# Linear attention in a fused decoder trunk: one of four projection blocks as a plain product, weight sums formed by accumulating loads, no weight split on GpSimd, gate activations issued later

## The chip, the cores and the metric

The kernel runs on one core of a Trainium2 chip. The metric is the time of one execution on the device in microseconds (us). A core has five engines with a queue each, which are named here as the profile names them: PE (matrix products; PEld are its weight loads), DVE (vector engine), ACT (scalar engine), POOL (GpSimd) and SP, which only issues transfers. POOL and ACT issue transfers too, and a transfer that adds to what lies at its destination is issued by POOL here. Each engine works its queue in order; an instruction that waits for a semaphore holds up all that stands behind it on its engine.

## The reference

Two layers on a sequence of 512 tokens, model width 1024, float32: latent attention and an MLP, then gated linear attention and an MLP, and a last norm. The change concerns the linear attention alone:

```python
def gla_mixer(xn, w_in, w_gk_up, b_gk, g_norm, w_o):
    h = xn @ w_in                       # w_in: 1024 x 3088
    q = h[..., :512]; k = h[..., 512:1024]          # 4 heads of 128
    v = h[..., 1024:2048]; g = h[..., 2048:3072]    # 4 heads of 256
    gk = log_sigmoid(h[..., 3072:] @ w_gk_up + b_gk) / 16
    ...                                 # chunks of 64, decays exp(cumsum(gk))
    o = rms_norm(o, g_norm)
    o = o * silu(g)
    return o.reshape(B, S, 1024) @ w_o
```

`...` stands for the recurrence over chunks: products of queries with the state, of queries with keys under the decay, and the new state.

## The kernel before, in words

Every matrix operand in float32 is cut into a high and a low part, and a product is three PE passes (high·high, high·low, low·high). The cut of a weight piece of 128x1024 is two instructions: ACT copies the high part (tile `wh`, line L124), and the difference (tile `wl`, L127) is a subtraction with two inputs from on-chip memory, on DVE or, where `lo_eng=POOL` is given, on POOL. `piece` (L164) does both.

The linear attention (`gla`, from L1243) computes the columns of q, k, v and g from the normed input X. The columns of v and g come in four blocks of 512 columns: v for heads 0 and 1 (called "v"), g for heads 0 and 1 ("g"), then "V" and "G" for heads 2 and 3. Before, each block is done by `b_type` with seven quadrant products in place of eight (Strassen's scheme in Winograd's form): the input and the weight are halved in both directions, sums of input quadrants (T1 to T4) are formed once by `quadrants` (L1257), and sums of weight quadrants for each block. A quadrant product (`product`, L1307) is 24 matmuls of 256 columns, all at L1314. The weight quadrants lie in four rooms of 128x1024: a11, s1, a12 and s3. Two of the four weight sums are formed while loading: SP loads one quadrant (L1303) and POOL then loads another on top of it (L1305). The other two are formed on DVE: a11 becomes s1 + a11 (L1344), a12 becomes a11 + a12 (L1355). Of the seven cuts of a block, four have their subtraction on DVE and three on POOL (`cut_in(a12, POOL)`, `cut_in(s3, POOL)`, `cut_in(a22, POOL)`). `copied` (L1317) and `added` (L1322) put the partial results together in the order that the scheme needs.

`v_done` (L1481, L1482) scales v by the row norms and cuts it; `g_done` (L1390) collects g in tiles and then, right at the end of the block, runs the eight gate activations (Silu, L1395) on ACT at high priority. They need another function table than the rest, so a table load stands ahead of them and one behind.

Two lists of work are woven into each other by hand (`proj` and `heads`, driven by the loop at the end of `gla`): `proj` yields units of main work (a product counts 0.7, a q or k column piece 2), and for every unit the loop takes 1.27 steps of `heads`. A step is a stage of the decay products of two heads (`levels`: on DVE the products L1542, L1574, L1575 and the masked copies L1559, L1561, L1584; on PE L1549 and L1599), or of `states`, `own_tiles`, `past` and `gated`, which form the outputs. For heads 0 and 1 the levels fall into "v" and "g", and states and outputs into the q and k pieces of the other two heads; for heads 2 and 3 the levels fall into "V" and "G", and the rest behind them. Then comes the output projection (`out_start`, `out_proj`), whose first three tiles need all heads.

The order on each engine is settled when the program is built; the PE order, above all, is fixed, so PE waits at a product whose operand is late even if a later one could run.

Of the kernel before, what the change touches and what calls it, by code (L numbers as in the profile page):

```python
# [18 lines left out]
P = 128  # L19
D = 1024  # L20
# [30 lines left out]
def trunk_kernel(ctx: ExitStack, tc: tile.TileContext, t_in: dict, out: bass.AP):  # L51
# [112 lines left out]
    def piece(raw, a, n, order=lambda i: i, at=(W_AT, W_AT), lo_eng=DVE):  # L164
        hi = room_for("wh", a, n, at[0])
        lo = room_for("wl", a, n, at[1])
        split(raw, hi, lo, lo_eng=lo_eng, order=order)
        return hi, lo
# [1074 lines left out]
    def gla(layer, nrm, vtag, ytag):  # L1243
# [13 lines left out]
        def quadrants():  # L1257
# [6 lines left out]
            sums = [[f(slot(vtag)) for _ in range(2)] for _ in range(4)]  # L1264
            t1, t2, t3, t4 = ([two[k // 2][:, k % 2 * TH : (k % 2 + 1) * TH] for k in lead] for two in sums)
            for k in lead:
                g1, g2 = (gcol(nrm.g, nrm.g0 + j) for j in (k, k + KH))
                u, v = xT[k], xT[k + KH]
                ACT.activation(t3[k], u[:, second], AF.Copy, scale=g1)
                DVE.scalar_tensor_tensor(t3[k], v[:, second], g2, t3[k], ALU.mult, ALU.subtract)  # L1270
                DVE.scalar_tensor_tensor(t2[k], u[:, first], g1, t3[k], ALU.mult, ALU.add)
                DVE.scalar_tensor_tensor(t4[k], v[:, first], g2, t2[k], ALU.mult, ALU.subtract)
                DVE.scalar_tensor_tensor(t1[k], v[:, second], g2, t2[k], ALU.mult, ALU.subtract)
            xr = residual_room("T12", F32R, 12).rearrange("p k (a t) -> p k a t", a=2)
            for n, (name, sign) in enumerate((("T1", -1.0), ("T2", -1.0), ("T3", 1.0), ("T4", -1.0))):
                quad[name] = []
                for i in range(2):
                    src = sums[n][i]
                    if n < 2:
                        parts = xr[:, n * KH + 2 * i : n * KH + 2 * i + 2]  # L1280
                        todo = [(parts[:, :, 0], parts[:, :, 1], src.rearrange("p (k t) -> p k t", k=2))]
                        quad[name] += [parts[:, k] for k in range(2)]
                    else:
                        todo = []
                        for k in range(2):
                            parts = slot(ytag).rearrange("p (a t) -> p a t", a=2)
                            todo.append((parts[:, 0], parts[:, 1], src[:, k * TH : (k + 1) * TH]))
                            quad[name].append(parts)
                    for hi, lo, x in todo:
                        ACT.activation(hi, x, AF.Copy, scale=sign)  # L1290
                        DVE.scalar_tensor_tensor(lo, x, sign, f(hi), ALU.mult, ALU.subtract)

        room = []

        def b_type(c0, hf, done, opens, c_next=None):
            def quadrant(base, c, h):
                cols = base + hf * 512 + c * TH
                return w_in[h * 512 : (h + 1) * 512, cols : cols + TH].rearrange("(k p) n -> p k n", p=P)

            def fetch(base, t, plain, more=None):  # L1300
                if base is None:
                    return
                SP.dma_start(t, quadrant(base, *plain))  # L1303
                if more:
                    POOL.dma_start(t, quadrant(base, *more), accum_op=ALU.add)  # L1305

            def product(o, w, name, start):  # L1307
# [17 lines left out]
            def cut_in(raw, lo_eng=DVE):  # L1325
                return piece(raw, KH, TH, at=AT_SEVEN, lo_eng=lo_eng)

            b0, b1, b2, b3 = bank("b"), bank("b"), bank("b"), bank("ac"[hf])
            if opens:
                two = [sb.tile([P, ND, TH], F32, tag="wraw", bufs=2, name=uname("wraw")) for _ in range(2)]  # L1330
                room[:] = [t[:, i * KH : (i + 1) * KH] for t in two for i in range(2)]
                z, w, y, w2 = b0, b1, b2, b3
            else:
                z, w, y, w2 = b2, b3, b1, b0
            a11, s1, a12, s3 = room
            a22 = s1
            if opens:
                fetch(c0, a11, (0, 0))
                fetch(c0, s1, (1, 1), (1, 0))
                fetch(c0, a12, (0, 1))  # L1340
                fetch(c0, s3, (1, 0), (0, 0))
            product(z, cut_in(a11), "11", True)
            copied(y, z)
            DVE.tensor_tensor(a11, s1, a11, ALU.add)  # L1344
            yield
            product(w, cut_in(s1), "T1", True)
            copied(w2, w)
            fetch(c0, a22, (1, 1))
            yield
            product(z, cut_in(a11), "T2", False)  # L1350
            u = copied(tmp(), z)
            yield
            product(y, cut_in(a12, POOL), "21", False)
            done(0, 0, y)
            DVE.tensor_tensor(a12, a11, a12, ALU.add)  # L1355
            fetch(c_next, a11, (0, 0))
            yield
# [3 lines left out]
            fetch(c_next, s3, (1, 1), (1, 0))  # L1361
            done(1, 1, added(w2, v))
            yield
            product(w, cut_in(a12), "22", False)
            fetch(c_next, a12, (0, 1))
            done(0, 1, added(w, u))
            yield
            product(z, p22, "T4", False)
            fetch(c_next, a22, (1, 0), (0, 0))
            done(1, 0, z)  # L1370
            room[:] = [a11, s3, a12, a22]
            yield
# [4 lines left out]
        def g_done(hf):  # L1377
# [7 lines left out]
            def done(c, th, p):  # L1385
# [7 lines left out]
                for n, s in enumerate(G[hf][: 2 * NT]):  # L1393
                    with tc.high_priority():
                        tc.keep_in_program_order(ACT.activation(s, s, AF.Silu, scale=rtok[:, n // 2 : n // 2 + 1]))  # L1395
                        if n == 2 * NT - 1:
                            exp_set()
# [8 lines left out]
            return done  # L1406

# [66 lines left out]
        def v_done(hf):  # L1474
            def done(c, th, p):
                hi, lo = V[2 * hf + c, th] = slot(vtag), slot(vtag)
                r_all = rtok_n if c else rtok
                for i in range(2):
# [3 lines left out]
                    DVE.scalar_tensor_tensor(lo[:, cs], p[:, cs], r, f(hi[:, cs]), ALU.mult, ALU.subtract)  # L1482
                if (c, th) == (1, 0):
                    vdone.add(hf)
# [163 lines left out]
        def head_values(h):  # L1648
            return [cut(V[h, j // 2], slice(None), slice(j % 2 * HV, (j % 2 + 1) * HV)) for j in range(NT)]
# [71 lines left out]
        def proj():  # L1721
            parts = {
                "v": lambda: b_type(2 * DK, 0, v_done(0), True, 2 * DK + D),
                "g": lambda: b_type(2 * DK + D, 0, g_done(0), False),
                "q": lambda: proj_qk(1),
                "k": lambda: proj_qk(3),
                "V": lambda: b_type(2 * DK, 1, v_done(1), True, 2 * DK + D),
                "G": lambda: b_type(2 * DK + D, 1, g_done(1), False),
            }
            for c in "vgqkVG":  # L1730
                for _ in parts[c]():
                    yield 2 if c in "qk" else 0.7


        def heads():
            for h in (0, 2):
# [27 lines left out]
                else:  # L1764
                    yield from run((states, 2), (own_tiles, 2), (past, 2), (states, 3))
                    while 1 not in gdone:
                        yield
# [148 lines left out]
```

## Time and profile before

| quantity | value |
|---|---|
| median of three runs | 1070.75 us (1069.05 to 1070.79) |
| profiled execution, its own time | 1071.23 us |
| its span, first to last instruction | 1069.5 us |
| PE busy in the span | 1033.5 us |
| DVE busy | 923.9 us |
| ACT busy | 726.3 us |
| POOL busy | 142.8 us |
| moved by transfers | 156.37 MB |

The table is read against the span: what PE is not busy is at most 36 us in all, and the linear attention, from about 495 to 720 us, holds most of it. The granted PE clock of the whole span is 0.984 of full speed. A duration in the trace is that of one instruction with its latency; since instructions on one engine overlap in a pipeline, the distance between two starts is shorter than the duration.

### The profile page before, as it was taken

How to read it: one execution, taken by the hardware profiler on the slowest of the kernel's cores; microseconds unless marked ns; L12 is line 12 of the kernel's file. 1: busy time of each engine (PE TensorE's matmuls, PEld its weight loads, DVE VectorE, ACT ScalarE, POOL GpSimd, SP SyncE). 2: the span in 40 equal slices, each digit the busy share in tenths (PEclk: the TensorE clock that was granted, in tenths of full speed). 3: DMA queues.
4: the chain of work that ended last, by engine and by line, in shares of the span. 5: the costliest groups of instructions: out<-in, count | busy, mean ns of one | idle time of the engine just before them, and what ended most of it. 6: DMA issues, size and time to landing. Idle time of an engine off the chain costs nothing.

```text
span 1069.5 us, 17680 instructions
## 1 busy us (share of the span) xinstructions
PE 1033.5 (97%) x6810; PEld 940.1 (88%) x6810; DVE 923.9 (86%) x1395; ACT 726.3 (68%) x1206; POOL 142.8 (13%) x164
## 2 busy tenths in 40 slices
PE   9999999999999999999988987799999999999997
PEld 7788888899999999998788877788899899889986
DVE  7889975999999898999988499569889989999994
ACT  7667754676787677676446573865676776777784
POOL 7410001200000010002203032200000100000000
PEclk9999999999999999999988998999999999999999
DMA  7401224778777768526343533543747777677422
GB/s 228 119 21 40 80 79 129 207 204 209 175 205 194 209 168 209 144 72 184 88 81 119 118 78 72 187 119 119 197 139 188 197 206 203 170 211 191 131 79 78
DMA packets 75011, 156.37 MB, mean 146 GB/s; under 512 B 10064, under 2 KB 46928, under 8 KB 72368
## 3 DMA queue, kind: packets, MB, share of 16 engines
q1 hardware_dynamic: 59264, 115.66, 33.6%
q0 software_dynamic: 13568, 37.75, 19.7%
q10 hardware_dynamic: 2096, 1.84, 0.5%
q8 instruction: 53, 0.87, 0.3%
q14 instruction: 30, 0.25, 0.1%
HBM read 150.78 MB, written 4.19 MB: 145 GB/s over the span
## 4 chain that ended last, share of the span: by engine, by line
PE 78%; DVE 11%; ACT 6%; issue 3%; DMA 2%; POOL 0%; SPq 0%; ACTq 0%; DVEq 0%; POOLq 0%
PE ps L992 24%; PE ps L1012 12%; PE ps L1005 12%; PE ps L132 6%; PE ps L133 6%; PE ps L134 6%; PE ps L1314 3%; DVE wl L127 2%; PE ps L1180 2%; PE ps L149 1%; PE ps L1214 1%; ACT wh L124 1%; DVE qk L1542 1%; PE ps L440 1%; DMA wraw<-in_gla_w_o_dram 1%
## 5 line engine op out<-in xcount | busy, mean ns | idle before, releaser
L124 ACT ACTIVATE wh<-wraw 128x1024 fp32r<-128x1024 f32 x151 | 158.4, 1055 | 96.4 <-issue 38.4
L127 DVE TENSOR_TENSOR wl<-wraw,wh 128x1024 fp32r<-128x1024 f32 x139 | 173.3, 1249 | 29.3 <-ACT wh L124 28.5
L992 PE MATMUL ps<-T,wh 128*128 128x256 f32 x896 | 154.6, 275 | 0.1
L127 DVE TENSOR_TENSOR wl<-comb,wh 128x1024 fp32r<-128x1024 f32 x112 | 136.6, 1221 | 14.4 <-ACT wh L124 14.4
L124 ACT ACTIVATE wh<-comb 128x1024 fp32r<-128x1024 f32 x112 | 118.5, 1058 | 43.3 <-issue 30.0
L992 PEld LDWEIGHTS ps<-T,wh 128*128 128x128 f32 x896 | 134.8, 188 | 0.3 <-ACT tmp L1022 0.3
L992 PE MATMUL ps<-T,wl 128*128 128x256 f32 x448 | 123.3, 275 | 0.0
L1012 PE MATMUL ps<-wh,set 128*128 128x512 f32 x392 | 122.1, 390 | 0.0
L992 PE MATMUL ps<-set,wh 128*128 128x256 f32 x672 | 116.9, 276 | 0.0
L132 PE MATMUL ps<-set,wh 128*128 128x512 f32 x280 | 109.8, 392 | 0.2 <-ACT set L1717 0.2
L133 PE MATMUL ps<-set,wh 128*128 128x512 f32 x280 | 109.6, 391 | 0.0
L134 PE MATMUL ps<-set,wl 128*128 128x512 f32 x280 | 109.3, 390 | 0.0
L1005 PE MATMUL ps<-hidden_parts,wh 128*128 128x256 f32 x784 | 105.9, 275 | 0.0
L992 PEld LDWEIGHTS ps<-set,wh 128*128 128x128 f32 x672 | 101.8, 188 | 0.5
L1005 PEld LDWEIGHTS ps<-hidden_parts,wh 128*128 128x128 f32 x784 | 96.7, 188 | 0.0
L992 PE MATMUL ps<-set,wl 128*128 128x256 f32 x336 | 92.5, 275 | 0.0
L1012 PEld LDWEIGHTS ps<-wh,set 128*128 128x128 f32 x392 | 73.6, 188 | 15.2
L992 PEld LDWEIGHTS ps<-T,wl 128*128 128x128 f32 x448 | 84.1, 188 | 0.0
L1012 PE MATMUL ps<-wl,set 128*128 128x512 f32 x196 | 76.3, 389 | 0.0
L1314 PE MATMUL ps<-wh,set 128*128 128x256 f32 x320 | 62.6, 289 | 1.1 <-ACT wh L124 1.1
L992 PEld LDWEIGHTS ps<-set,wl 128*128 128x128 f32 x336 | 63.1, 188 | 0.0
L132 PEld LDWEIGHTS ps<-set,wh 128*128 128x128 f32 x280 | 52.6, 188 | 11.1 <-ACT set L1717 0.4
(452 smaller groups left out, 2362.3 us busy)
## 6 DMA issues: line engine op xcount, KB each, us to landing
comb<-in_mlp_w_down_dram SPq DMA_DIRECT2D x74, 512.0 KB, 4.5
wraw<-in_mlp_w_up_dram SPq DMA_DIRECT2D x18, 1024.0 KB, 4.9
wraw<-in_mlp_w_up_dram SPq DMA_DIRECT2D x28, 512.0 KB, 5.7
comb<-in_mlp_w_down_dram POOLq DMA_DIRECT2D x28, 512.0 KB, 6.5
wraw<-in_gla_w_in_dram SPq DMA_DIRECT2D x20, 512.0 KB, 3.8
comb<-in_mlp_w_up_dram SPq DMA_DIRECT2D x14, 512.0 KB, 4.7
comb<-in_mlp_w_up_dram POOLq DMA_DIRECT2D x14, 512.0 KB, 6.2
wraw<-in_mlp_w_up_dram POOLq DMA_DIRECT2D x14, 512.0 KB, 7.2
```

The lines of the kernel that those rows point to most:

```text
L124: order(ACT.activation(hi, src, AF.Copy))
L127: lo_eng.tensor_tensor(lo, src, f(hi), ALU.subtract)
L132: PE.matmul(psum, wh, xh, start=start, stop=False)
L133: PE.matmul(psum, wh, xl, start=False, stop=False)
L134: PE.matmul(psum, wl, xh, start=False, stop=stop)
L149: PE.transpose(psum, src, ident[: src.shape[0], : src.shape[0]])
L440: PE.matmul(p, w[:, i, j * P : (j + 1) * P], x, start=start, stop=stop)
L992: PE.matmul(o, a_, x_, start=start and j == 0 and k == 0 and n == 0, stop=k == KH - 1 and n == 2, skip_group_check=True)
L1005: PE.matmul(o, w_[:, k, j * P : (j + 1) * P], x_[:, ts], start=opens, stop=k == 1 and n == 2, skip_group_check=True)
L1012: PE.matmul(o, x_, w_, start=start and k == 0 and n == 0, stop=k == 1 and n == 2, skip_group_check=True)
L1180: PE.matmul(p, a, x, start=k == 0 and n == 0, stop=k == 3 and n == 2)
L1314: PE.matmul(p, x_, w_[:, k], start=start and t == 0 and k == 0 and n == 0, stop=k == KH - 1 and n == 2, skip_group_check=True)
```

## The change

Four things change, all in `gla`. The block "v" is computed by a new `b_type` as a plain product: eight row pieces of 128, 512 columns at a time, 96 matmuls of 512 columns and four weight cuts. The other three blocks keep the seven products, under the name `seven`. In `seven` all four weight sums come from loads: a fifth room, E, holds the sums for the products T2 and 22; it is filled by a plain load and two accumulating ones, and by one more between T2 and 22 (`fetch_more`). For E two halves of 128x512 are taken from the buffers of tag `acc`. The rooms change their parts from "V" to "G". All cuts have their subtraction on DVE (`lo_eng` is gone). The Silus leave `g_done` and become a step `silu(hf)` of `heads`: for heads 0 and 1 after both heads' own tiles, for heads 2 and 3 ahead of `gated`, without high priority. `quadrants` becomes a generator whose steps are taken two before the gates and the others during "v". A step without units counts 2.45 (before 2).

```diff
@@ quadrants
-            sums = [[f(slot(vtag)) for _ in range(2)] for _ in range(4)]
+            sums = gp.tile([P, 2 * NT * HV], F32, tag="g", bufs=1, name="x_sums").rearrange("p (i k t) -> p i k t", i=2, k=KH)
...
             for k in lead:
...
+                for name, src, sign in (("T3", t3, 1.0), ("T4", t4, -1.0)):
+                    parts = slot(ytag).rearrange("p (a t) -> p a t", a=2)
+                    parted((parts[:, 0], parts[:, 1]), src, sign)
+                    quad[name].append(parts)
+                yield
+            xr = residual_room("T12", F32R, 12).rearrange("p (i k) (a t) -> p i k a t", i=2, a=2)
+            for i, name in enumerate(("T1", "T2")):
+                parted((xr[:, i, :, 0], xr[:, i, :, 1]), sums[:, i], -1.0)
...
+        def b_type(c0, hf, done):
+            banks = [bank("b"), bank("b"), bank("b"), bank("ac"[hf])]
+            def mms(w, kk, k, t):
+                xk = cut(X[k], slice(None), slice(t * P, (t + 1) * P))
+                mm3(banks[t], xk, cut(w, slice(None), kk), k == 0, k == ND - 1)
+            for kc in range(2):
+                raw = load(...)
+                for g in range(2):
+                    w = piece(raw[:, 2 * g : 2 * g + 2], 2, 512, at=AT_SEVEN)
...
+        def fetch(base, buf, *terms):
+            for part, t in enumerate(buf):
+                for n, q in enumerate(terms):
+                    src = quadrant(base, *q, part if len(buf) > 1 else None)
+                    if n:
+                        POOL.dma_start(t, src, accum_op=ALU.add)
+                    else:
+                        SP.dma_start(t, src)
+        SUM_1, SUM_2, SUM_3 = ((1, 1), (1, 0)), ((1, 1), (1, 0), (0, 0)), ((1, 0), (0, 0))
...
             product(z, cut_in(a11), "11", True)
             copied(y, z)
-            DVE.tensor_tensor(a11, s1, a11, ALU.add)
+            fetch(base, a11, (1, 1))
+            a22 = a11
...
-            product(z, cut_in(a11), "T2", False)
+            product(z, cut_in(both), "T2", False)
+            fetch_more(base, both)
...
-            product(y, cut_in(a12, POOL), "21", False)
+            product(y, cut_in(a12), "21", False)
             done(0, 0, y)
-            DVE.tensor_tensor(a12, a11, a12, ALU.add)
-            fetch(c_next, a11, (0, 0))
+            if after:
+                fetch(after, a12, *SUM_1)
...
-            p3, p22 = cut_in(s3, POOL), cut_in(a22, POOL)
-            product(z, p3, "T3", False)
+            product(z, cut_in(s3), "T3", False)
...
-            product(w, cut_in(a12), "22", False)
+            product(w, cut_in(both), "22", False)
...
+        def fetch_more(base, buf):
+            for part, t in enumerate(buf):
+                POOL.dma_start(t, quadrant(base, 0, 1, part if len(buf) > 1 else None), accum_op=ALU.add)
@@ g_done
-                for n, s in enumerate(G[hf][: 2 * NT]):
-                    with tc.high_priority():
-                        tc.keep_in_program_order(ACT.activation(s, s, AF.Silu, scale=rtok[:, n // 2 : n // 2 + 1]))
-                        if n == 2 * NT - 1:
-                            exp_set()
+        def silu(hf):
+            for n, s in enumerate(G[hf][: 2 * NT]):
+                tc.keep_in_program_order(ACT.activation(s, s, AF.Silu, scale=rtok[:, n // 2 : n // 2 + 1]))
+            exp_set()
@@ proj
-                "v": lambda: b_type(2 * DK, 0, v_done(0), True, 2 * DK + D),
-                "g": lambda: b_type(2 * DK + D, 0, g_done(0), False),
+                "v": lambda: b_type(2 * DK, 0, v_done(0)),
+                "g": lambda: seven(2 * DK + D, 0, g_done(0), ahead=2 * DK + FB),
...
-                "V": lambda: b_type(2 * DK, 1, v_done(1), True, 2 * DK + D),
-                "G": lambda: b_type(2 * DK + D, 1, g_done(1), False),
+                "V": lambda: seven(2 * DK + FB, 1, v_done(1), after=2 * DK + D + FB),
+                "G": lambda: seven(2 * DK + D + FB, 1, g_done(1)),
@@ heads
-                    yield from run((states, 0), (own_tiles, 0), (states, 1), (own_tiles, 1), (past, 0), (gated, 0))
+                    yield from run((states, 0), (own_tiles, 0), (states, 1), (own_tiles, 1))
+                    silu(0)
+                    yield from run((past, 0), (gated, 0))
```

Three places show how this moves instructions. On POOL, these are the rows for the blocks "v" and "g" before (`wraw_6210` and `wraw_6211` hold the rooms, `wl` are low parts):

```order
L1305 DMA wraw_6211<-in_gla_w_in_dram 128x4x256
L127 TENSOR_TENSOR wl_6323<-wraw_6211,wh_6322 128x1024
L127 TENSOR_TENSOR wl_6373<-wraw_6211,wh_6372 128x1024
L127 TENSOR_TENSOR wl_6377<-wraw_6210,wh_6376 128x1024
L1305 DMA wraw_6211<-in_gla_w_in_dram 128x4x256
L1305 DMA wraw_6210<-in_gla_w_in_dram 128x4x256
L127 TENSOR_TENSOR wl_6657<-wraw_6211,wh_6656 128x1024
```

In the changed program POOL holds no L127 in the linear attention, and its queue from "g" to the start of "V" reads as follows (`weight_sum_6075` and `weight_sum_6076` are the halves of E, `wraw_6441`, `wraw_6442`, `wraw_7098` and `wraw_7099` hold the other rooms, L1424 is `fetch_more`):

```order
L1332 DMA wraw_6441<-in_gla_w_in_dram 128x4x256
L1332 DMA wraw_6442<-in_gla_w_in_dram 128x4x256
L1424 DMA weight_sum_6075<-in_gla_w_in_dram 128x2x256
L1424 DMA weight_sum_6076<-in_gla_w_in_dram 128x2x256
L1332 DMA weight_sum_6075<-in_gla_w_in_dram 128x2x256
L1332 DMA weight_sum_6076<-in_gla_w_in_dram 128x2x256
L1332 DMA weight_sum_6075<-in_gla_w_in_dram 128x2x256
L1332 DMA weight_sum_6076<-in_gla_w_in_dram 128x2x256
L1332 DMA wraw_7098<-in_gla_w_in_dram 128x4x256
L1332 DMA wraw_7099<-in_gla_w_in_dram 128x4x256
```

What moved: twelve subtractions left POOL's queue, and its accumulating loads in `gla` went from 8 to 22, four of which stand between E's use in "g" and the first sum of "V" (`wraw_7098`).

On DVE, the second place is the start of "g", whose cuts now all stand there between the levels of heads 0 and 1 (L1608 is L1542 of the kernel before); before, this stretch held four cuts, the adds L1344 and L1355 and the masked copies:

```order
L127 TENSOR_TENSOR wl_6450<-wraw_6441,wh_6449 128x1024
L127 TENSOR_TENSOR wl_6480<-wraw_6441,wh_6479 128x1024
L1608 TENSOR_TENSOR qk_6158<-qk_6158,T_6168 128x2x32x8
L127 TENSOR_TENSOR wl_6520<-weight_sum_6075,wh_6519 128x512
L1608 TENSOR_TENSOR qk_6158<-qk_6158,T_6168 128x2x16x16
L127 TENSOR_TENSOR wl_6520<-weight_sum_6076,wh_6519 128x512
L1608 TENSOR_TENSOR qk_6027<-qk_6027,T_6124 128x2x8x32
L127 TENSOR_TENSOR wl_6564<-wraw_6442,wh_6563 128x1024
L1608 TENSOR_TENSOR qk_6158<-qk_6158,T_6168 128x2x8x32
L127 TENSOR_TENSOR wl_6607<-wraw_6442,wh_6606 128x1024
```

What moved: three cuts per block came to DVE from POOL, two adds per block left it, and the levels stand a little nearer to the cuts they share the queue with.

On ACT, the third place is the end of "G". Before, the eight Silus with their two table loads stand ahead of `kth`, the high part of the turned keys, for which PE needs the states of heads 2 and 3:

```order
L1390 ACTIVATE g_7655<-ps_7490 128x256
L1395 ACT_TABLE_LOAD
L1395 ACTIVATE g_7654<-g_7654,rtok 128x256 x3
L1395 ACTIVATE g_7655<-g_7655,rtok 128x256 x3
L1395 ACTIVATE g_7656<-g_7656,rtok 128x256 x2
L139 ACT_TABLE_LOAD
L124 ACTIVATE kth_7821<-ps_7817 128x384
```

In the changed program `kth` stands ahead of the last cuts of the block, and the Silus stand behind the state parts (`S`) and the first two gathers (L1783), ahead of the squares of `gated` (L1762) and of the third gather:

```order
L124 ACTIVATE S_7809<-tmp_7805 128x256
L1783 ACTIVATE set_7840<-ps_7835,gains 128x512
L124 ACTIVATE S_7814<-tmp_7812 128x256
L1457 ACT_TABLE_LOAD
L1457 ACTIVATE g_7604<-g_7604,rtok 128x256 x3
L1457 ACTIVATE g_7605<-g_7605,rtok 128x256 x3
L1457 ACTIVATE g_7606<-g_7606,rtok 128x256 x2
L139 ACT_TABLE_LOAD
L1762 ACTIVATE tmp_7845,gms_7844<-ps_7766 128x256
L1783 ACTIVATE set_7876<-ps_7871,gains 128x512
```

What moved: the Silus went from ahead of the states of heads 2 and 3 to behind them. For heads 0 and 1 they went from the end of "g" to behind both heads' own tiles, where on ACT the cut of the second weight room of "V" (`wh_7150<-wraw_7098`, the accumulated sum) now stands a few rows ahead of them.

More of the change, by code (lines that the diff above doesn't have):

```diff
@@ L1275, in quadrants @@
[L1275 to L1282, printed above, removed]
-                    else:
[L1284 to L1305, printed above, removed]
+                t = tmp()
@@ L1307, in product, with spread_room, seven @@
+        SUM_1, SUM_2, SUM_3 = ((1, 1), (1, 0)), ((1, 1), (1, 0), (0, 0)), ((1, 0), (0, 0))
+        def spread_room():
+            room["E"] = [sb.tile([P, S], F32, tag="acc", bufs=2, name=uname("weight_sum")).rearrange("p (k n) -> p k n", n=TH) for _ in range(2)]
+        def seven(base, hf, done, after=None, ahead=None):
             def product(o, w, name, start):
@@ L1648, in head_values @@
         def head_values(h):
-            return [cut(V[h, j // 2], slice(None), slice(j % 2 * HV, (j % 2 + 1) * HV)) for j in range(NT)]
+            return [V[h, j] for j in range(NT)]
         def tile_of(pair, i):
```

129 lines of the change are left out of this document (93 added, 36 removed).

## The prediction

> **What bounds the kernel now.** I read the page first, then windows by stage, then PE's waits, then the timeline around the waits.
>
> ```profile
> span 1069.5 us, 17680 instructions
> PE 1033.5 (97%) x6810; PEld 940.1 (88%) x6810; DVE 923.9 (86%) x1395; ACT 726.3 (68%) x1206; POOL 142.8 (13%) x164
> ```
>
> PE is busy for 1033.5 of 1069.5 us, so all its gaps hold 36 us. The next fence gives windows: bounds, length, then busy time and count of PE, PEld, DVE, ACT and POOL, the granted clock, the DMA share and GB/s. The first four are "v" with "g"; q, k, states and outputs of heads 0 and 1; "V" with "G"; and what follows until three tiles of the output projection are done.
>
> ```profile
> 495.80:587.50 91.70, 81.89 (x518) 74.82 (x517) 81.28 (x155) 52.83 (x98) 21.67 (x14) 0.93 0.43 104
> 587.50:619.00 31.50, 31.00 (x169) 26.32 (x167) 16.31 (x28) 19.36 (x44) 2.58 (x2) 1.00 0.48 109
> 619.00:683.50 64.50, 54.21 (x401) 51.81 (x400) 59.36 (x117) 37.77 (x77) 21.99 (x16) 0.92 0.46 125
> 683.50:719.70 36.20, 30.27 (x168) 26.18 (x167) 18.67 (x44) 25.18 (x62) 1.75 (x2) 0.91 0.43 114
> 688.40:693.30 4.90, 0.01 (x1) 0.00 (x0) 0.01 (x1) 4.87 (x11) 0.00 (x0) 0.79 0.01 5
> 693.30:697.30 4.00, 3.99 (x18) 3.90 (x19) 3.01 (x6) 2.59 (x6) 0.00 (x0) 0.50 0.07 12
> 621.60:623.60 2.00, 0.04 (x1) 0.04 (x1) 2.00 (x5) 0.58 (x1) 1.36 (x1) 1.00 0.00 0
> 623.60:627.60 4.00, 4.00 (x35) 4.00 (x36) 4.00 (x14) 3.59 (x8) 0.71 (x1) 1.00 0.25 62
> 425.00:450.00 25.00, 25.00 (x223) 25.00 (x222) 22.71 (x24) 16.76 (x23) 1.73 (x2) 1.00 0.61 175
> 725.00:750.00 25.00, 25.00 (x112) 20.69 (x111) 22.55 (x35) 13.01 (x21) 0.00 (x0) 1.00 0.36 127
> ```
>
> Call the first four A, B, C and D. Idle PE is 9.8, 0.5, 10.3 and 5.9 us. A lower clock also costs time: busy time by what the clock lacks is 81.9 x 0.07 = 5.7, 0, 54.2 x 0.08 = 4.3 and 30.3 x 0.09 = 2.7. The losses are A 15.5, B 0.5, C 14.6 and D 8.6, together 39 us. That is the pot this change can draw from. The two pairs below the stages show how gap and clock belong together: behind a gap of 4.9 us the clock is 0.50 over 4 us (2.0 lost), behind one of 2.0 us it stays 1.00. The last two rows give the pace of matmuls without waits: 25/223 = 0.112 us for 256 columns and 25/112 = 0.223 for 512.
>
> PE's waits from 495 to 720 us (waiting line, what ended the wait, total, times, longest):
>
> ```profile
> PE ps L1549 <- ACT q L1556: 7.9, 3, 5.5
> PE ps L132 <- ACT kth L124: 5.4, 2, 4.9
> PE ps L1314 <- DVE wl L127: 3.7, 3, 1.9
> PE ps L1549 <- DVE q L1575: 2.3, 1, 2.3
> PE ps L1314 <- ACT wh L124: 2.3, 4, 0.7
> PE ps L1314 <- DVE g L1698: 2.0, 1, 2.0
> ```
>
> Levels late (7.9 + 2.3), weight cuts late (3.7 + 2.3), and one wait of 4.9 us for `kth`, which the Silus hold up on ACT. DVE is busy 81.3 of 91.7 us in A and 59.4 of 64.5 in C, so it is the pacer there. What makes DVE slow is seen in its timeline (start, duration):
>
> ```profile
> 564.36 5.66 POOL L127 TENSOR_TENSOR wl<-wraw,wh 128x1024 fp32r<-128x1024 f32 x2 [24.43 <-DVE A L1584]
> 564.55 3.23 DVE L127 TENSOR_TENSOR wl<-wraw,wh 128x1024 fp32r<-128x1024 f32 x1
> 567.85 2.72 DVE L1542 TENSOR_TENSOR qk<-qk,T 128x512 f32<-128x512 f32 x1
> 570.49 1.21 DVE L127 TENSOR_TENSOR wl<-wraw,wh 128x1024 fp32r<-128x1024 f32 x1
> 538.64 1.29 POOL L1305 DMA_DIRECT2D wraw<-in_gla_w_in_dram  x1 [1.30 <-DMA wraw<-in_gla_w_in_dram]
> 538.44 0.69 DVE L1537 TENSOR_TENSOR qk<-q,T 128x512 f32<-128x512 f32 x1 [0.17 <-ACT T L143]
> ```
>
> Beside POOL's cuts a DVE cut takes 3.23 us and just after them 1.21; L1542 takes 2.72. The last pair is a POOL issue of an accumulating load beside a DVE product of the same size as L1542: 0.69, not stretched.
>
> **The change part by part.** Rows by group, and for tile T with minimum/median/maximum in ns:
>
> ```profile
> L124 ACT ACTIVATE wh<-wraw 128x1024 fp32r<-128x1024 f32 x38 | 39.6, 1052 | 15.9 <-PE ps L133 13.0 <-DMA wraw<-in_gla_w_o_dram 1.4 <-DVE wraw L1344 1.2
> L127 DVE TENSOR_TENSOR wl<-wraw,wh 128x1024 fp32r<-128x1024 f32 x26 | 35.6, 1375 | 8.9 <-ACT wh L124 8.8
> L127 POOL TENSOR_TENSOR wl<-wraw,wh 128x1024 fp32r<-128x1024 f32 x12 | 30.6, 2557 | 85.8 <-ACT wh L124 29.1 <-DVE A L1584 24.4 <-DVE T L1502 15.9
> L1542 DVE TENSOR_TENSOR qk<-qk,T 128x512 f32<-128x512 f32 x28 | 23.1, 829 | 0.9 <-ACT E L1591 0.9
> L1395 ACT ACTIVATE g<-g,rtok 128x256 f32<-128x256 f32 x16 | 6.6, 496 | 0.0
> L1322 DVE TENSOR_TENSOR tmp<-ps,tmp 128x512 f32<-128x512 f32 x8 | 5.5, 685 | 0.2
> L1355 DVE TENSOR_TENSOR wraw<-wraw,wraw 128x1024 f32<-128x1024 f32 x4 | 4.9, 1215 | 1.8 <-POOL wl L127 1.8
> ```
>
> ```profile
> L1542 DVE TENSOR_TENSOR qk<-qk,T x28: 672/684/2761, 542.1 to 679.8; 128x512 f32<-128x512 f32 x28
> L1574 DVE TENSOR_TENSOR q<-qk,T x8: 409/435/2393, 542.9 to 655.7; 128x256 f32<-128x256 f32 x8
> L1575 DVE TENSOR_TENSOR q<-q,T x8: 272/278/2434, 545.7 to 656.1; 128x128 f32<-128x128 f32 x8
> ```
>
> [...] L127 loses 26 x (1375 - 1215) = 4.2 us and L1542 28 x (829 - 684) = 4.1. One L1574 and one L1575 lose 2.0 and 2.2. Smaller forms stand beside POOL's cuts as well: those listed lose 12.5 us, and POOL is there 30.6 us, which is the upper end (12.5 to 30.6). I take 20, near the middle: the forms not listed are short and hit less often. With DVE's wait for POOL (1.8) it is 22, about 11 in A and 11 in C.
>
> [...]
>
> *Cuts and adds on DVE.* In A "v" has four cuts where four were on DVE, "g" seven for four: +3 x 1.215; four adds (L1344, L1355) leave: -4 x 1.215. Two L1322 fewer, at 0.685, give -1.4. A: 3.6 - 4.9 - 1.4 - 11 = -13.7 us. In C: +6 cuts, -4 adds, 7.3 - 4.9 - 11 = -8.6 us.
>
> *Plain "v" on PE.* Seven products of 24 at 0.112 are 18.8 us; 96 x 0.223 are 21.4. **+2.6 us**, with no cover, as PE is what waits least. Fewer dependent steps come with it.
>
> *Accumulating loads.* L1305 stands at 1.31 us (row below), so 14 more occupy POOL for 18.3 us, against 30.6 that go. POOL's time is free unless a load is late (rivals). The added loads of some 6.8 MB (13 of 0.5 MB) make 30 GB/s more over 224 us, on a DMA share of 0.43 to 0.48 in the stages; I cost them at nothing while that share leaves half.
>
> ```profile
> L1305 POOL DMA_DIRECT2D wraw<-in_gla_w_in_dram x8: 1277/1309/1352, 494.5 to 643.0; - x8
> DMA to landing us min/median/max: 5.9/6.0/8.0
> ```
>
> *Silus.*
>
> ```profile
> 686.87 1.28 ACT L1395 ACT_TABLE_LOAD   x1
> 688.16 3.30 ACT L1395 ACTIVATE g<-g,rtok 128x256 f32<-128x256 f32 x8
> 691.48 1.28 ACT L139 ACT_TABLE_LOAD   x1
> ```
>
> 5.9 us on ACT each time. For heads 2 and 3 the wait for `kth` goes (4.9 + 2.0 of clock = 6.9), but the Silus then stand ahead of `gated` and of the third gather, on which the output projection waits; little of PE's work lies between, so I let 4.4 come back: gain 2.5 (bounds 0 and 6.9). For heads 0 and 1 they go from B, where PE loses 0.5 us, to just ahead of "V", whose banks `gated` frees and whose cuts queue behind them: I charge 2 (bounds 0 and 5.9 + 2.0).
>
> *What PE gets.* In A, PE without losses needs 91.7 - 15.5 + 2.6 = 78.8 us and DVE 81.3 - 13.7 = 67.6, so DVE no longer fills it. What stays late is the start of the levels, a chain over DVE, ACT and PE: of the 15.5 I leave 5.9 (the wait of 5.5 and rest). Gain 15.5 - 5.9 - 2.6 = 7.0; bounds 0 and 12.9. In C, PE needs 64.5 - 14.6 = 49.9 and DVE 59.4 - 8.6 = 50.8: equal, so waits stay. I take 6.5 of 8.6, less the 2 of the Silus: 4.5; bounds -2 and 13.7. In B the cut of q's first weights waits for a room that "g" frees later: -1 (bounds 0 and -6, one landing). Sum: 7.0 - 1 + 4.5 + 2.5 = **13 us**.
>
> [...]
>
> **The rivals.**
> 1. *Forecast*, 1071.2 - 13 = 1058.
> 2. *The waits go altogether*: A 12.9, B 0.5, C 64.5 - 50.8 = 13.7, D 6.9, together 34: 1037; halfway 1047. For: DVE's relief is large. Against: in C DVE then has no slack at all, and the chain at the start of the levels is longer than DVE's share in it.
> 3. *`fetch_more` is late.* Between T2 and 22 lie three products, 3 x 24 x 0.112 = 8.1 us. Two issues (2.6), landing (6.0 to 8.0) and the cut on ACT and DVE (1.05 + 1.22) are 10.9 to 12.9. Levels woven in lengthen the cover. If PE waits the mean 3.8 in three blocks, 11 us go: 1069, or 1066 if one block is covered.
> 4. *It does not do what it says*: POOL's issues hinder DVE as its cuts did. Then 18.3/30.6 of 22 us, 13, return and the time stays at 1071. Against: 0.69 us beside an issue, and eight issues within 1277 to 1352 ns although DVE is busy. [...]
> 5. *Slower: POOL's queue is too long for "V".* Four accumulations into E and the first sum of "V" stand in order, each waiting for the landing before: five at 1.31 + 6.0 = 7.3 to 9.3 us, 37 to 47. The cover is B and three products, 31.5 + 8.1 = 39.6, so it decides above 7.9 us each. At 9.3 the cut is 6.9 late; on ACT the states and Silus queue behind it (5.9), the gap halves the clock (2.0), and the same lateness meets the next sums of "V" and "G" (2 x 3.8): 1058 + 22 = 1080. Against: the two halves go in turn, so their landings overlap.
>
> **How the numbers follow.** Forecast 0.58 (its own range 1051 to 1064), the waits go 0.12, `fetch_more` late 0.14, no relief 0.07, POOL's queue 0.09. Faster: 0.58 + 0.12 + 0.14 = 0.84; same 0.07; slower 0.09, with 0.2% (2 us) about what a measurement of this kernel can tell from no change. Range: 1046 (half of rival 2) to 1069 (rival 3 within). The profiled execution is 0.5 us above the median of 1070.75, which I leave in.
>
> **What would show it.** Right: no DVE product of 128x512 over 0.8 us between "v" and "G"; clock 1.00 in most of A; no wait of PE for `kth`; A some 7 us shorter, C 4.5. Wrong: waits of seven's line for a cut of E (rival 3), an ACT wait for the weight room of "V" (5), issues over 1.5 us or stretched DVE rows beside them (4), or PE waiting for the levels as long as before, since then DVE was not what made them late.

## The result and the profile after

The changed kernel takes 1062.15 us (median of four runs, 1061.44 to 1063.0), against 1070.77 beside it: ratio 0.9922, 95% interval 0.9904 to 0.9939. It is faster by 8.6 us; 1058 was forecast, within 1046 to 1069. The first lines of its page:

```profile
span 1061.0 us, 17531 instructions
PE 1032.9 (97%) x6738; PEld 937.0 (88%) x6738; DVE 902.4 (85%) x1393; ACT 721.8 (68%) x1198; POOL 128.6 (12%) x166
```

PE is busy as long as before (1032.9 against 1033.5 us): the gain is idle time. The windows are cut at the same places of the program as A, B and C in the prediction ("v" and "g"; q, k and outputs; "V" and "G"), with the same columns:

```profile
495.60:581.40 85.80, 82.12 (x450) 71.47 (x449) 71.69 (x150) 49.08 (x89) 12.38 (x13) 0.96 0.52 124
581.40:611.20 29.80, 29.80 (x161) 25.62 (x160) 14.07 (x26) 18.25 (x42) 5.39 (x5) 1.00 0.66 149
611.20:679.30 68.10, 55.55 (x408) 54.12 (x407) 51.95 (x126) 41.30 (x85) 12.42 (x15) 0.90 0.65 153
659.30:672.20 12.90, 9.21 (x80) 8.97 (x78) 4.01 (x5) 3.95 (x9) 4.31 (x8) 1.00 0.90 292
643.70:648.60 4.90, 1.58 (x9) 1.39 (x9) 4.20 (x10) 1.96 (x6) 0.00 (x0) 0.65 0.00 0
648.60:652.60 4.00, 4.00 (x23) 4.00 (x23) 4.00 (x6) 1.49 (x5) 0.47 (x1) 0.57 0.46 135
668.50:673.80 5.30, 0.01 (x1) 0.00 (x0) 0.47 (x1) 1.55 (x3) 0.00 (x0) 0.88 0.97 333
673.80:677.80 4.00, 3.96 (x18) 3.96 (x19) 4.00 (x6) 3.77 (x8) 0.00 (x0) 0.50 0.03 10
```

A shrank from 91.7 to 85.8 us and B from 31.5 to 29.8, while **C grew from 64.5 to 68.1**. What follows C (span less its end) went from 1069.5 - 683.5 = 386.0 to 1061.0 - 679.3 = 381.7. Together 5.9 + 1.7 - 3.6 + 4.3 = 8.3 us, and 0.2 stood ahead of A. In C the loss rose although DVE is busy for 52.0 us in place of 59.4: PE is idle for 12.6 us there and loses an estimated 5.6 more by the granted clock of 0.90 (55.55 x 0.10). PE's waits from 495 to 720 us:

```profile
PE ps L1665 <- ACT E L1657: 7.6, 3, 3.3
PE ps L1349 <- ACT tmp L1352: 5.3, 1, 5.3
PE ps L132 <- ACT set L1783: 3.1, 1, 3.1
PE ps L1615 <- ACT q L1639: 1.2, 1, 1.2
PE ps L1349 <- DVE wl L127: 1.0, 1, 1.0
PE ps L1615 <- ACT q L1622: 0.7, 2, 0.6
PE ps L1615 <- DVE q L1641: 0.4, 1, 0.4
```

The wait for `kth` is gone, and those for weight cuts fell from 6.0 us to 1.0. Those for the levels have hardly fallen: 7.6 + 1.2 + 0.7 + 0.4 = 9.9 us (L1665 and L1615) against the 10.2 quoted before, most of them now for the tile E of the levels, a copy on ACT (L1657), which shares only its name with the weight room E. The wait of 5.3 us is read from the timelines of ACT, SP and POOL (start, duration, what ended the wait):

```profile
662.65 0.66 ACT L1442 ACTIVATE g<-ps 128x256 f32<-128x256 f32 x2
672.25 1.06 ACT L124 ACTIVATE wh<-wraw 128x1024 fp32r<-128x1024 f32 x1 [8.94 <-DMA wraw<-in_gla_w_o_dram]
673.21 0.58 ACT L1352 ACTIVATE tmp<-ps 128x512 f32<-128x512 f32 x1
660.44 16.71 SPq L154 DMA_DIRECT2D wraw<-in_gla_w_o_dram  x3
659.33 4.31 POOL L1451 DMA_DIRECT2D xT_back<-kept_x  x8 [5.92 <-PE ps L1349]
673.84 0.58 PE L1349 MATMUL ps<-wh,set 128*128 128x256 f32 x1 [5.33 <-ACT tmp L1352]
```

ACT waits 8.94 us for the first load of the output projection's weights, to cut it. Right behind stands the copy L1352 of a bank to which the last product of "G" adds; its operand, the product T3, had been ready since about 665. The load was issued at 660.44, 1.1 us after the first of eight loads of `xT_back` (2 MB on POOL's queue), and landed 11.8 us later, while the transfers were busy for 0.90 of the time.

What the prediction said of DVE is in the forms of tile T, and of POOL in the lines of its accumulating loads (minimum/median/maximum, ns):

```profile
L1608 DVE TENSOR_TENSOR qk<-qk,T x28: 672/687/742, 538.3 to 657.1; 128x512 f32<-128x512 f32 x28
L1641 DVE TENSOR_TENSOR q<-q,T x8: 270/285/342, 539.8 to 638.2; 128x128 f32<-128x128 f32 x8
```

```profile
L1332 POOL DMA_DIRECT2D weight_sum<-in_gla_w_in_dram x8: 1189/1198/1706, 504.9 to 628.3; - x8
L1332 POOL DMA_DIRECT2D wraw<-in_gla_w_in_dram x7: 1274/1293/1311, 520.6 to 631.6; - x7
```

```profile
L1424 POOL DMA_DIRECT2D weight_sum<-in_gla_w_in_dram x4: 1189/1200/1708, 560.2 to 610.1; - x4
```

No product is stretched any more (maxima of 742 and 342 ns against 2761 and 2434). The issues for the rooms of 128x1024 stay as they were; of those for the halves of E, which come in pairs, the longest took 1706 and 1708 ns.

One more wait stands in ACT's timeline, for a sum that "G" needs (its last accumulating load was issued at 631.60):

```profile
638.62 1.06 ACT L124 ACTIVATE wh<-wraw 128x1024 fp32r<-128x1024 f32 x1 [3.01 <-DMA wraw<-in_gla_w_in_dram]
```

Right behind this cut ACT makes the copy L1639 for which PE waits 1.2 us, and the waits of 2.0 and 3.3 us for E follow within 10 us. That the late sum brings them about is read from this order; no run takes it away alone.

### The profile page after: what moved, and what is told of

It is laid out like the page before. It is cut to its first block, busy times and chain, and to the rows that moved or that the text cites. A ratio compares the mean times of both kernels' runs of the same rounds, so it can differ in the third digit from the quotient of the medians.

```text
span 1061.0 us, 17531 instructions
## 1 busy us (share of the span) xinstructions
PE 1032.9 (97%) x6738; PEld 937.0 (88%) x6738; DVE 902.4 (85%) x1393; ACT 721.8 (68%) x1198; POOL 128.6 (12%) x166
## 2 busy tenths in 40 slices
DMA packets 78867, 161.09 MB, mean 152 GB/s; under 512 B 10336, under 2 KB 49760, under 8 KB 76224
## 4 chain that ended last, share of the span: by engine, by line
PE 82%; DVE 10%; ACT 5%; DMA 2%; issue 1%; ACTq 0%; SPq 0%; DVEq 0%
PE ps L992 24%; PE ps L1012 13%; PE ps L1005 13%; PE ps L133 7%; PE ps L134 7%; PE ps L132 6%; PE ps L1349 3%; PE ps L1180 2%; DVE wl L127 2%; PE ps L1214 1%; PE ps L149 1%; DMA wraw<-in_gla_w_o_dram 1%; PE ps L440 1%; ACT wh L124 1%; DVE qk L1608 1%
## 5 line engine op out<-in xcount | busy, mean ns | idle before, releaser
L124 ACT ACTIVATE wh<-wraw 128x1024 fp32r<-128x1024 f32 x143 | 150.3, 1056 | 111.5 <-PE ps L133 39.0
L127 DVE TENSOR_TENSOR wl<-wraw,wh 128x1024 fp32r<-128x1024 f32 x143 | 174.5, 1222 | 37.2 <-ACT wh L124 36.4
L127 DVE TENSOR_TENSOR wl<-comb,wh 128x1024 fp32r<-128x1024 f32 x112 | 136.7, 1221 | 14.4 <-ACT wh L124 14.4
L992 PEld LDWEIGHTS ps<-set,wh 128*128 128x128 f32 x672 | 102.0, 188 | 0.5
L132 PEld LDWEIGHTS ps<-set,wh 128*128 128x128 f32 x280 | 52.8, 189 | 14.5 <-ACT set L1783 3.5
L133 PEld LDWEIGHTS ps<-set,wh 128*128 128x128 f32 x280 | 53.0, 189 | 11.8 <-DVE set L1784 0.5
```

Of the source, the lines that this page charges most:

```text
L124: order(ACT.activation(hi, src, AF.Copy))
L127: lo_eng.tensor_tensor(lo, src, f(hi), ALU.subtract)
L132: PE.matmul(psum, wh, xh, start=start, stop=False)
L133: PE.matmul(psum, wh, xl, start=False, stop=False)
L992: PE.matmul(o, a_, x_, start=start and j == 0 and k == 0 and n == 0, stop=k == KH - 1 and n == 2, skip_group_check=True)
```

## Experiments

Each was timed beside runs of the kernel before (medians 1070.0 to 1070.8); ratios are to that kernel, with 95% intervals.

### What POOL's cuts cost

The kernel before, with its twelve POOL cuts on DVE and nothing else changed (e6):

```diff
-            def cut_in(raw, lo_eng=DVE):
-                return piece(raw, KH, TH, at=AT_SEVEN, lo_eng=lo_eng)
+            def cut_in(raw, lo_eng=None):
+                return piece(raw, KH, TH, at=AT_SEVEN)
```

> The kernel before with all its twelve POOL cuts subtracted on DVE, nothing else changed. Theory (the stretch of DVE beside POOL's cuts, some 22 us, costs more than the cuts themselves, 12 x 1.22 = 14.6 us): 2 to 6 us faster than before. Rival (DVE is the pacer, and 14.6 us more on it weigh as much as the stretch): within 1.5 us of before, or slower.

Measured: **1058.74 us, 0.9894 (0.9881 to 0.9907)**. That is beyond the 2 to 6 us of the theory. One of the change's four parts, alone, brings 11.3 us, and all four together 8.6: as built, the other three cost 3.4 us (their intervals just touch). DVE's busy time in the whole span is 914.6 us against 923.9, with twelve cuts of 1.22 more, so the stretch that went is estimated at 9.3 + 14.6 = 24 us. Its windows of A and C:

```profile
495.80:579.40 83.60, 77.46 (x518) 70.02 (x517) 77.59 (x159) 51.38 (x96) 5.89 (x7) 1.00 0.46 111
611.40:667.60 56.20, 51.61 (x403) 50.46 (x402) 50.34 (x121) 35.04 (x73) 6.90 (x10) 0.97 0.48 130
```

A is 8.1 us shorter than before and C 8.3, though DVE's busy time in A fell by only 3.7 us (81.3 to 77.6): the stretch hit the instructions that PE was waiting for. PE was idle for 6.1 us in A and 4.6 in C (9.8 and 10.3 before), and the granted clock was 1.00 and 0.97 (0.93 and 0.92 before). PE's waits for the levels are down to some 6 us, the largest row being:

```profile
PE ps L1549 <- DVE q L1575: 5.6, 2, 3.2
```

The other way round, nine cuts of the changed kernel back on POOL, 21, T3 and T4 of each of three blocks (e1; `cut_in` hands the engine on to `split`):

```diff
-            product(y, cut_in(a12), "21", False)
+            product(y, cut_in(a12, POOL), "21", False)
-            product(z, cut_in(s3), "T3", False)
+            product(z, cut_in(s3, POOL), "T3", False)
-            product(z, cut_in(a22), "T4", False)
+            product(z, cut_in(a22, POOL), "T4", False)
```

> The changed kernel with three of the seven cuts of each quadrant block (21, T3, T4) subtracted on POOL again. Theory (POOL's cuts held DVE up): 9 cuts of about 2.5 us come back on POOL, DVE products beside them are stretched to over 2 us again, 16 us of stretch against 9 x 1.22 = 11 us of cuts that leave DVE; the time rises by 3 to 7 us over the changed kernel (1065 to 1069). Rival (the plain block and the loaded sums made the gain, the place of the cuts none): within 1 us of the changed kernel, or faster, since DVE has nine cuts fewer.

Measured: 1067.38 us, 0.9965 (0.9951 to 0.9979), 5.2 us slower than the changed kernel. The row of tile T and the group row show why:

```profile
L1608 DVE TENSOR_TENSOR qk<-qk,T x28: 679/685/3039, 537.6 to 662.2; 128x512 f32<-128x512 f32 x28
```

```profile
L1608 DVE TENSOR_TENSOR qk<-qk,T 128x512 f32<-128x512 f32 x28 | 25.1, 895 | 4.4 <-ACT E L1657 4.4
```

The median is unchanged and the maximum is 3039 ns: a few of 28 are hit, and they make 5.8 us (28 x (895 - 687)). In the whole span DVE is busy for 907.4 us against 902.4, although nine cuts (11.0 us) left it: 16 us of stretch, as expected. Both pairs of runs say the same: DVE was busy for less time with twelve or nine cuts more and none on POOL beside it (914.6 against 923.9 us, 902.4 against 907.4).

### What happened in "V" and "G"

First, the cuts of the output projection's weights stand on ACT behind the last copy of g, which `copied_g` keeps; transfers as in the changed kernel (e9):

```diff
-                    begun.append(out_start(w_o, Y, 3, "bca"))
+                    with tc.issue_after(copied_g[1].ins):
+                        begun.append(out_start(w_o, Y, 3, "bca"))
```

> The changed kernel with the cuts of the output projection's first weights placed on ACT behind the last copy of g, so that the copy for the last product of G does not stand behind a cut that waits for a transfer. Theory (ACT's order carries the transfer's lateness to PE): the wait of 5.3 us goes, 4 to 7 us faster than the changed kernel (1055 to 1058), the transfer itself still takes 11 to 12 us. Rival (PE needs the cut weights soon after, so the wait only moves): within 1.5 us.

Measured: **1056.35 us, 0.9863 (0.985 to 0.9877)**, 5.8 us faster than the changed kernel. The transfer is as slow (landings up to 11.9 us), but no copy stands behind it:

```profile
671.57 0.66 ACT L1443 ACTIVATE g<-ps 128x256 f32<-128x256 f32 x2 [1.74 <-PE ps L1349]
672.62 1.06 ACT L124 ACTIVATE wh<-wraw 128x1024 fp32r<-128x1024 f32 x1 [0.40 <-DMA wraw<-in_gla_w_o_dram]
```

ACT's wait for the load is 0.40 us in place of 8.94, since it has the copies to do meanwhile, and C ends at 671.5 in place of 679.3:

```profile
611.20:671.50 60.30, 52.60 (x409) 51.43 (x408) 48.69 (x122) 38.42 (x82) 12.35 (x15) 0.94 0.67 155
```

C is 60.3 us long, 4.2 shorter than before the change.

Second, the loads of `xT_back` should start later, by a write into their room that waits for the state parts of head 2. At first the write went into one of eight columns (e4; `bring_back` is called behind `silu(1)` and takes the place of the lines in `g_done`):

```diff
+        def bring_back():
+            x = residual_room("xT_back")
+            ...
+            DVE.tensor_copy(x[:, 0, :1], f(AT[2]["S"][0][0][:, :1]))
+            for j in range(ND):
+                POOL.dma_start(x[:, j], kept[:, j])
```

> The changed kernel with the eight loads of xT_back (2 MB on POOL's queue) held until the first state parts of head 2, some 20 us later. Theory (they slow the first load of the output projection's weights, which ACT waits 8.9 us for ahead of a copy that PE needs): that load lands in 5 to 7 us in place of 11.8, PE's wait of 5.3 us before the last product of G falls under 1.5 and the time by 4 to 7 us (1055 to 1058). Rival (the load is late because its room is free late): landing stays near 12, no gain.

Measured: 1060.26 us, 0.9908 (0.9893 to 0.9922). It tells nothing of the theory, since POOL's timeline shows seven of the loads issued as early as ever:

```profile
657.33 3.78 POOL L1455 DMA_DIRECT2D xT_back<-kept_x  x7 [6.18 <-PE ps L1349]
679.71 0.54 POOL L1455 DMA_DIRECT2D xT_back<-kept_x  x1 [18.59 <-DVE xT_back L1453]
```

With a write into every column, `x[:, :, 0]` (e4b):

> As e4, with all eight loads of xT_back held (in e4 seven of them stood ahead of the one that waits, and started when they had before). Theory (2 MB beside it slow the first 1 MB load for the output projection): it lands in 5 to 7 us after its issue, PE's wait before the last product of G falls under 1.5 us, and the time is 4 to 7 us under the changed kernel. Rival (the load is slow or late for another reason): landing near 12 us and the time within 2 us of the changed kernel.

Measured: **1053.84 us, 0.9846 (0.9832 to 0.9859)**, 8.3 us faster than the changed kernel. The line of its four weight loads, and a window from where the loads of `xT_back` began in the changed kernel:

```profile
L154 SPq DMA_DIRECT2D wraw<-in_gla_w_o_dram x4: 368/368/368, 659.3 to 673.4; - x4
DMA to landing us min/median/max: 5.0/5.1/6.1
```

```profile
659.30:664.40 5.10, 5.10 (x46) 5.10 (x45) 2.91 (x5) 2.87 (x7) 0.00 (x0) 1.00 0.78 259
```

The loads land in 5.0 to 6.1 us (5.0 to 12.3 in the changed kernel), PE is never idle in those 5.1 us, and the wait before the last product is gone. Two edits that share nothing but this wait each remove it: the transfer was late because of its neighbour, and ACT's order brought the lateness to PE. Why e4b gains 2.5 us more than e9 stays open; their intervals overlap.

What brought the two transfers together is seen in e6, the kernel before with nothing but its cuts moved:

```profile
655.08 4.33 POOL L1404 DMA_DIRECT2D xT_back<-kept_x  x8 [25.14 <-PE ps L1314]
656.93 16.36 SPq L154 DMA_DIRECT2D wraw<-in_gla_w_o_dram  x3
668.43 1.06 ACT L124 ACTIVATE wh<-wraw 128x1024 fp32r<-128x1024 f32 x1 [3.78 <-DMA wraw<-in_gla_w_o_dram]
```

There too `xT_back` begins ahead of the weights (in the kernel before it began 5.1 us behind them), the weights take up to 11.7 us to land, and ACT waits. But the copy for the last product of "G" stands ahead of that cut on ACT (at 661.12), and PE does not wait there. So moving the cuts is enough to change the order of the loads, and the place of the weight cut on ACT makes PE pay.

### The Silus

Silus of heads 2 and 3 back at the end of "G" in the changed kernel (e2; the lines left out are the eight Silus and `exp_set`, as before):

```diff
+                if hf in (1,):
+                    ...
                 gdone.add(hf)
-                    silu(1)
```

> The changed kernel with the Silus of heads 2 and 3 at the end of G again, the rest unchanged. Theory (their move took a wait out of the chain of the states): the state parts of heads 2 and 3 queue behind 5.9 us on ACT, PE waits about 4 us there and the wait of 3.1 us at the third gather goes; 1 to 4 us slower than the changed kernel. Rival (the Silus cost the same wherever they stand after G): within 1 us.

Measured: 1061.81 us, 0.992 (0.9908 to 0.9933): the rival's number. As the late transfer lies at the same place, the edit was made on top of e9 too (e12):

> e9 (cuts of the output projection's first weights behind the last copy of g) with the Silus of heads 2 and 3 back at the end of G. Theory (the Silus' move is worth something once the transfer's wait is out of ACT's way): 2 to 4 us slower than e9, with PE waiting for the state parts. Rival (their 5.9 us cost the same on either side of the states, as the third gather waits for them there): within 1 us of e9.

Measured: 1056.16 us, 0.9868 (0.9852 to 0.9885), against 1056.35 without it. PE's waits show that the time only changes its place; the Silus back at the end of "G":

```profile
PE ps L1748 <- ACT S L124: 4.0, 2, 2.8
```

and with them where the change put them:

```profile
PE ps L132 <- ACT set L1784: 3.4, 1, 3.4
```

In both programs the cut of `kth` stands ahead of the Silus on ACT, since the steps of heads 2 and 3 come earlier relative to "G" than before. So it is not the Silus' own move that took the wait for `kth` away. The new weave is the likely cause; no run puts the old one back.

Silus of heads 0 and 1 back at the end of "g" (e3, the same edit with `(0,)` and `silu(0)`):

> The changed kernel with the Silus of heads 0 and 1 at the end of g again. Theory (as charged in the prediction, their new place ahead of V costs 2 us): 1 to 3 us faster than the changed kernel. Rival (ACT has slack at both places): within 1 us.

Measured: 1060.19 us, 0.9907 (0.9891 to 0.9924; single runs from 1057.15 to 1062.72). The interval overlaps the changed kernel's, so 2 us is possible and not shown.

### The plain block

"v" in seven quadrant products again, all input sums formed ahead of it (e5):

```diff
-        next(forming)
-        next(forming)
+        for _ in forming:
+            pass
-                "v": lambda: b_type(2 * DK, 0, v_done(0)),
+                "v": lambda: seven(2 * DK, 0, v_done(0), after=2 * DK + D),
```

> The changed kernel with the block v in seven quadrant products again, its sums by accumulating loads and all four input sums formed ahead of it. Theory (the plain block costs 2.6 us on PE, but removes the chain of accumulating loads, three cuts and the forming of the input sums from ahead of the levels): 1 to 5 us slower than the changed kernel, with PE waiting in v for cuts or sums. Rival (the plain block only costs PE): 2 to 3 us faster.

Measured: 1076.84 us, 1.0065 (1.005 to 1.008), 14.7 us slower than the changed kernel, far outside the 1 to 5 expected, and slower than the kernel before. PE's waits:

```profile
PE ps L1556 <- DVE tmp L1521: 6.7, 1, 6.7
PE ps L1349 <- ACT tmp L1352: 6.3, 2, 5.3
PE ps L1613 <- DVE q L1639: 5.1, 1, 5.1
PE ps L1349 <- ACT T L1269: 3.4, 1, 3.4
```

The first stands ahead of "v": ACT waits 8.88 us for the accumulated sum in E and holds up the gates behind it; the last is the forming of the input sums. So it is no clean price of the plain block (the kernel before made these sums another way), but it shows what the plain "v" gives the accumulating loads: time ahead of "g".

"V" plain as well, on top of e9 (e13; `v_done` by tile, and "g" loads ahead for "G"):

```diff
-                "V": lambda: seven(2 * DK + FB, 1, v_done(1), after=2 * DK + D + FB),
+                "V": lambda: b_type(2 * DK, 1, v_done(1)),
```

> e9 with the block V plain as well, so that two blocks are plain and G opens its own rooms. Theory (in V and G DVE is the pacer: busy 47 of 50 us there): three cuts fewer on DVE (3.7 us) and no chain of sums into G, against 2.6 us on PE and four cuts that G loads late; 0 to 4 us faster than e9. Rival (PE paces after all, or G's first sums arrive late): 2 to 5 us slower than e9.

Measured: **1048.06 us, 0.9788 (0.9773 to 0.9802)**, another 8.3 us, twice the upper end of what was expected. PE's waits for the levels' tile E fall from 7.6 us to one:

```profile
PE ps L132 <- ACT set L1783: 3.1, 1, 3.1
PE ps L1665 <- ACT E L1657: 2.4, 1, 2.4
```

The one that is left lies in "g"; "V" and "G" have none. The edit takes away three cuts and also the sums that "V" handed on to "G", so the run doesn't tell which of the two made the levels late.

With the late loads of `xT_back` on top (e15):

> Three edits together on the changed kernel: cuts of the output projection behind the last copy of g (e9), V plain (e13), loads of xT_back held (e4b). Theory (the waits that e13 has left are not the transfer's): 1046 to 1049, 0 to 2 us under e13. Rival (e4b gave more than e9, and that part comes on top): 1043 to 1046.

Measured: 1047.9 us, 0.9796 (0.9784 to 0.9809): nothing more to gain from that transfer, as its theory had it. And all four blocks plain, with e9's cuts (e16; `g_done` by tile; x isn't set aside and brought back, as no room of it is taken):

```diff
-                "g": lambda: seven(2 * DK + D, 0, g_done(0), ahead=2 * DK + FB),
+                "g": lambda: b_type(2 * DK + D, 0, g_done(0)),
-                "V": lambda: seven(2 * DK + FB, 1, v_done(1), after=2 * DK + D + FB),
+                "V": lambda: b_type(2 * DK, 1, v_done(1)),
-                "G": lambda: seven(2 * DK + D + FB, 1, g_done(1)),
+                "G": lambda: b_type(2 * DK + D, 1, g_done(1)),
```

> All four blocks plain, on the changed kernel with e9's order of cuts: no input sums, no weight sums, no accumulating loads, and x is neither set aside nor brought back. PE gets 2 x 2.6 us more than in e13 (28 products of 2.70 us become 4 x 21.4), DVE loses about 12 cuts of 1.22 us and the forming of the sums, and the transfers lose the sums and 4 MB. Theory (with the plain block the waits of V and G go, not only of v): 1044 to 1050, about e13. Rival (PE's extra passes are not covered, as PE was already busy nearly throughout in e13): 1050 to 1054.

Measured: 1047.88 us, 0.9792 (0.9779 to 0.9805). From its page, and its longest wait of PE from 495 to 720 us:

```profile
PE 1031.8 (99%) x6522; PEld 924.1 (88%) x6522; DVE 877.6 (84%) x1343; ACT 701.7 (67%) x1154; POOL 92.5 (9%) x128
```

```profile
PE ps L149 <- DVE set L1778: 4.4, 1, 4.4
```

Busy PE rose by 3.7 us against the kernel with two plain blocks (1028.1 there), and the waits that are gone pay for it. The three last versions are the fastest, 22 us under the kernel before, and can't be told apart.

## Why the prediction came out right, point by point

- **The stretch of DVE beside POOL's cuts.** Right, and shown from both sides: +5.2 us with nine cuts back on POOL, -11.3 us for moving twelve off it in the kernel before. The 20 us taken for the stretch were a fair size (some 24 in e6). Taking the cuts from it to get some 7 was too coarse: the time fell by 11.3, because the stretch sat on operands that PE waited for. What in the two engines makes the stretch, no run shows. In the changed kernel DVE's busy time fell by 9.6 us in A (13.7 forecast) and by 7.4 in C (8.6).
- **A, gain of 7.0.** Measured 5.9. PE's 2.6 us for the plain "v" would fit: with the cuts alone moved A takes 83.6 us, with the whole change 85.8; no run has the plain "v" alone.
- **B, -1.** Measured +1.7: PE is busy throughout B, so the first weights of q came in time.
- **C, gain of 4.5: this is the step that failed**, at -3.6. The prediction priced transfers by the mean share of a stage, put them at nothing while half of it was free, and thought only of the added ones (it put these at 6.8 MB; the whole program moves 161.09 MB in place of 156.37). What cost the time were loads that both kernels have: those of `xT_back` now began ahead of the weight loads instead of behind them (671.25 and 666.19 before, 659.33 and 660.44 after), the share was 0.90 for 13 us, and a cut in ACT's queue passed the delay on to PE. The two runs that removed the wait gave 5.8 and 8.3 us back, and in the first of them C gains 4.2 us, close to the 4.5.
- **D, gain of 2.5.** Measured 4.3, for another reason than the one given: the Silus' move is worth nothing (1056.16 against 1056.35), and the cut of `kth` stands ahead of them at either place. The bound of 0 for the move was the right value. For heads 0 and 1 the charge of 2 us is open.
- **The rivals.** `fetch_more` late: in "G" ACT waited 0.67 us for it and PE not at all. POOL's issues as a hindrance: no product is stretched beside them (742 ns at most), though the longest of the issues for E, 1706 and 1708 ns, passed the 1.5 us named as a sign. POOL's queue too long for "V": its first products waited for nothing, but a sum of "G" was 3.01 us late on ACT, as this rival had it for the next sums. The waits going altogether: not here, but the all-plain version comes near it.
- **A sign that came out against it.** PE's waits for the levels staying as long as before was to mean that DVE was not what made them late. They did stay (10.2 and 9.9 us). But e6 has some 6, so the stretch of DVE was part of it, and the rest of the change brought new lateness: the late sum on ACT stands ahead of the levels, and where "V" hands no sums on to "G" (e13, e15, e16) PE waits for no level there.
- That the time came within 4.2 us of the forecast is in part luck: A, B and what follows C gained 11.9 us, 3.4 more than forecast, and C took 3.6 back where it should have gained 4.5.

## What to carry to other kernels

A subtraction moved to an idle engine isn't free if work on the busy engine is stretched beside it, as a DVE product of 128x512 was here (2761 ns against a median of 684): price that stretch at the places where the bound engine waits, not in the mean. When an edit brings a transfer forward, look for what it now runs beside (a load landed in 11.8 us here beside 2 MB on another queue), and for the in-order queue in which a wait for a transfer stands ahead of work that is ready; moving that wait back gave 5.8 us here. A scheme that saves 12% of a block's passes (168 matmuls of 256 columns against 96 of 512) has to be weighed against the sums, cuts and loads it brings: here four plain blocks took 1047.9 us, against 1056.35 with three of them in seven products and the same order of cuts. And a change of several parts is worth taking apart: one part alone did at least as well as all four.

## What the runs showed of the hardware

The first 1 MB load of the output projection's weights, on SP's queue, landed 11.8 us after its issue beside 2 MB on POOL's queue in the changed kernel; in e4b, where those 2 MB were issued from 674.66 on, behind the last of the four weight loads (673.4), all four landed in 5.0 to 6.1 us. The prediction's two gaps left open what one between 2.0 and 4.9 us does to the granted clock: in the changed kernel, behind a wait of 3.3 us, with another of 2.0 and 0.7 us of matmuls shortly before it, it was 0.57 over 4 us (window 648.60), nearly as deep as behind one of 5.3 (0.50). Beside a subtraction on POOL a DVE product of 128x512 took up to 2761 ns in the kernel before and 3039 in e1, and 742 at most in the changed kernel, where none stands beside it.
